# The entry of a gate/up stage: five blocks begun ahead of the left factors, weights prepared by GpSimd, normed rows kept in the projection's tile

## The chip, the cores and the metric

The kernel runs on one core of a Trainium2 chip, in one launch. The metric is the device time of one execution in microseconds. A core has TensorE (PE, matmuls out of SBUF into PSUM), VectorE (DVE), ScalarE (ACT), GpSimd (POOL) and SyncE (SP, which issues most DMAs here). Each works off its own list of instructions in order, and waits on semaphores where it needs another's result.

## The reference

One layer of a streaming encoder on 512 tokens of width 2048, all float32: four token mixers side by side, cross-attention into 256 memory tokens, and a SwiGLU feed-forward of width 5632, each between two RMS norms.

```python
def swiglu_ffn(h, w_gu, w_down):
    gate, up = jnp.split(h @ w_gu, 2, axis=-1)
    return (jax.nn.silu(gate) * up) @ w_down
...
        x = x + rmsnorm(xa, g[XA_POST])
        x = x + rmsnorm(swiglu_ffn(rmsnorm(x, g[FFN_PRE]), ffn_w_gu[l], ffn_w_down[l]), g[FFN_POST])
```

The change lies between the last projection of the attention (which gives `xa`) and the first product of `h @ w_gu`.

## The kernel before

Every float32 factor is split in two parts for TensorE: a high part in the rounded format fp32r, made by a cast on ScalarE (names `whi`, `L` first half), and a low part, source minus high part, made by a subtraction on VectorE (`wlo`, `L` second half). `split3` (L991, L992) does this for one tile of 128 x 1024.

The attention's output projection is `y_proj`. It leaves its result in the tile `y` (four row tiles of 128 tokens, 2048 wide). It runs for the token tiles in two pairs, 0 and 1, then 2 and 3. After each pair, `advance_t` adds the residual (L953, the new x goes to DRAM at L956 by a DMA on GpSimd's queue), takes the squares for the next norm (`sumsq`, L242, on ScalarE), finds the inverse root by a row of small VectorE operations (L148 to L153; "root" below), scales the rows (L963 on ScalarE, L964 on VectorE), and transposes them on TensorE through PSUM (L970). VectorE evicts the transposes with the norm's gain (L972) into the tiles `xT` (named `stg`, `sa12` and so on).

`gate_up` computes h @ w_gu by a scheme with seven products in place of eight, on halves of the inner dimension, of the tokens, and of gate and up. Products are numbered 1 to 7. Each takes a left factor (`L[m]`, the tokens' side: a half of `xT` or a sum of halves, split in two parts) and a right factor (a half of a weight block or a sum of halves). The output's 5632 columns go in 44 blocks `j` of 128. One product of a block is 16 matmuls (`product`, L1088 and L1090, a high part by 512 columns and a low part by 256, eight times). A block's products 1 and 2 only need the first pair of token tiles (L1, L2), so they can be done before the second pair is normed: `begin(j)` does that and finishes the gate's first half, through one tile `f_x`. It holds one of the five PSUM banks named `mm` until `block(j)` takes over with products 6, 5, 7, 3 and 4. Three blocks are begun in `phase2` (pool `early`), blocks 3 and 4 inside `gate_up`.

Block 0 is run in steps together with the left factors 5, 6, 7, 4 and 3 (`left_parts`: four sums for each of two halves, then `split3`), since its own products use them first. Its right factors come from `right_parts` (sums at L1030, L1033, L1035, L1037) and `split_w`. Raw weights come by SP's queue, 512 KB a tile, into rings of three.

The order on each engine is set by a scheduler that interleaves the emitted instructions; the code gives the dependencies and the order of emission. The pools give how far something can run ahead.

Of the kernel before, what the change touches and what calls it, by code (L numbers as in the profile page):

```python
# [7 lines left out]
F32 = mybir.dt.float32  # L8
# [7 lines left out]
P = 128  # L16
# [53 lines left out]
def build(tc, x, mem, norm_g, w_in, conv_a_w, pool_w, pool_scale, gdn_conv_w, gdn_A_log,  # L70
# [824 lines left out]
    def phase2(act):  # L895
        with ExitStack() as s0:
            pp = pool("ptp", stack=s0)
            pt = [tuple(pp.tile([P, 4, T], F32R, name=f"pt{s}{i}") for s in "hl") for i in range(2)]
            with ExitStack() as s1:
                pl = pool("atp", stack=s1)  # L900
                for h in range(XH):
                    qh = pl.tile([P, 4, T], F32R, name="at_qh", bufs=2)
                    ql = pl.tile([P, 4, T], F32R, name="at_ql", bufs=2)
                    proj_a(act, xa_wq, h * XHD, lambda j, o: split(qh[:, j], ql[:, j], o), 2)
                    ks = slice(2 * (h % 2), 2 * (h % 2) + 2)
                    attention(h, qh, ql, pl, pt[h // 2][0][:, ks], pt[h // 2][1][:, ks])
                    if h == 0:
                        value_out(3, pl)
            es_act.close()
            ep = pool("early", 2, "right", es_early)  # L910
            sa12 = pool("sa12", 2, "right", es_a12)
            sa22 = pool("sa22", 2, "right", es_a22)
            stg = pool("stg", 4, "right", es_stg)
            yp = pool("yp2", stack=s0)
            pl2 = pool("adp2", stack=s0)
            xT = [[[p.tile([P, 4, 256], F32, name="stg") for _ in range(2)] for p in q]
                  for q in ((stg, stg), (sa12, sa22))]
            L = {m: [ep.tile([P, 4, 2, 256], F32R, name=f"L{m}") for _ in range(2)] for m in (1, 2)}
            begun = {}

            def then(i):
                def f(y, ss):
                    advance_t((2 * i, 2 * i + 1), y, ss, xT, pl2)
                    if i == 0:
                        for sub in range(2):
                            split3(pair(L[1][sub]), xT[0][0][sub])
                            split3(pair(L[2][sub]), xT[1][0][sub])
                    else:
                        for j in range(3):
                            begun[j] = begin(j, L, ep)  # L930
                return f
            y_proj(pt, vw_d, 3, yp, [(0, range(NT), None)] + [
                (c, range(2 * i, 2 * i + 2), then(i) if c == 3 else None) for i in range(2) for c in (1, 2, 3)])
        return xT, L, begun

    def advance_t(tiles, y, ss, xT, pl):


        xs = []
        for t in tiles:  # L940
            xt = pl.tile([P, D], F32, name="ad_x", bufs=2)
            nc.sync.dma_start(xt, x1_d[t * P:(t + 1) * P])
            xs.append(xt)
        s = sm.tile([P, 2], F32, name="rs_s")
        for i, t in enumerate(tiles):
            nc.vector.tensor_reduce(s[:, i:i + 1], ss[:, t], axis=AX.X, op=ALU.add)
        r = sm.tile([P, 2], F32, name="rs_r")
        mean_rsqrt(r, s, 2, D)
        sq = sm.tile([P, 2, 2], F32, name="nr_q")
        for i, t in enumerate(tiles):  # L950
            for hf in range(2):
                qs = slice(hf * 1024, (hf + 1) * 1024)
                nc.vector.scalar_tensor_tensor(xs[i][:, qs], y[:, t, qs], r[:, i:i + 1], xs[i][:, qs],  # L953
                                               op0=ALU.mult, op1=ALU.add)
                sumsq(xs[i][:, qs], sq[:, i, hf:hf + 1], pl)
            nc.gpsimd.dma_start(x2_d[t * P:(t + 1) * P], xs[i])  # L956
        s2 = sm.tile([P, 2], F32, name="nr_s2")
        nc.vector.tensor_reduce(s2, sq, axis=AX.X, op=ALU.add)
        n = sm.tile([P, 2], F32, name="nr_r2")
        mean_rsqrt(n, s2, 2, D)  # L960
        for hf in range(2):
            qs = slice(hf * 1024, (hf + 1) * 1024)
            nc.scalar.activation(xs[0][:, qs], xs[0][:, qs], AF.Copy, scale=n[:, 0:1])  # L963
            nc.vector.tensor_scalar(xs[1][:, qs], xs[1][:, qs], n[:, 1:2], None, op0=ALU.mult)  # L964
        for q in (0, 2, 1, 3):
            for i, t in enumerate(tiles):
                tp = ps.tile([P, 4, P], F32, name="ps")
                for j in range(4):
                    k = q * 4 + j
                    nc.tensor.transpose(tp[:, j], xs[i][:, k * P:(k + 1) * P], ident)  # L970
                o = t % 2 * P
                nc.vector.tensor_tensor(xT[q // 2][t // 2][q % 2][:, :, o:o + P], tp,  # L972
                                        bc(PA[:, 5 * 16 + q * 4:5 * 16 + q * 4 + 4], P), op=ALU.mult)

# [5 lines left out]

    ORDER = (1, 2, 6, 5, 7, 3, 4)
    FIRST = (5, 6, 7, 4, 3)

    def pair(t):

        return t[:, :, 0], t[:, :, 1]

    def split3(hl, src):  # L990
        nc.scalar.copy(hl[0], src)  # L991
        nc.vector.tensor_tensor(hl[1], src, hl[0].bitcast(F32), op=ALU.subtract)  # L992

    def left_parts(A11, A12, A21, A22, tmp, L, order):

# [24 lines left out]
                sums(3)  # L1020
            yield m

    def right_parts(B11, B12, B21, B22, new, order):

        tt = nc.vector.tensor_tensor
        s = {}
        for m in order:
            if m in (5, 6) and 5 not in s:
# [11 lines left out]
    def gate_up(xT, L, begun):  # L1040

        with ExitStack() as s0:
            def factor(name, *ms):
                lp = pool(name, 2, stack=s0, reuse_waits="tile")
                for m in ms:
# [6 lines left out]
            parts = [left_parts(xT[0][0][sub], xT[1][0][sub], xT[0][1][sub], xT[1][1][sub],  # L1052
                                tmp.tile([P, 4, 256], F32, name="tmp"),
                                Lazy(lambda m, sub=sub: pair(L[m][sub])), FIRST) for sub in range(2)]
            first = block(0, L, rp, tp, begun[0], FIRST)

            def step():
                for g in parts:
# [1 line left out]
                next(first)  # L1060
            step()
            step()
            begun[3] = begin(3, L, tp)
            step()
            es_stg.close()
            es_tmp.close()
            factor("lp4", 4)
            step()
            begun[4] = begin(4, L, tp)
            es_a22.close()  # L1070
            factor("lp3", 3)
            step()
# [19 lines left out]
    def fold(dst, src):  # L1092
        nc.vector.tensor_tensor(dst, src[:, 0:256], src[:, 256:512], op=ALU.add)

    def split_w(src):
        w = wp.tile([P, 8, P], F32R, name="whi"), wp.tile([P, 8, P], F32R, name="wlo")
        split3(w, src)
        return w

    def begin(j, L, pl):  # L1100


        A = mm.tile([P, 512], F32, name="mm")
        X, g = pl.tile([P, T], F32, name="f_x", bufs=1), pl.tile([P, 256], F32, name="f_g", bufs=3)
        for m, kh in ((2, 1), (1, 0)):
            b = wp.tile([P, 8, P], F32, name="raw")
            nc.sync.dma_start(b, w_gu[j, kh, 0])
            product(A, split_w(b), L, m)
            if m == 2:
                nc.scalar.copy(X, A)  # L1110
        gate(g, A, X)
# [7 lines left out]
        nc.scalar.activation(th, g, AF.Tanh, scale=0.5)  # L1119
        nc.vector.scalar_tensor_tensor(g, th, 1.0, g, op0=ALU.add, op1=ALU.mult)  # L1120

    def block(j, L, rp, tp, begun, order):

        q = {}
        for kh, g in ((0, 0), (1, 0), (0, 1), (1, 1)):
# [1 line left out]
            nc.sync.dma_start(q[kh, g], w_gu[j, kh, g])  # L1127
        tl = lambda n, w=T: tp.tile([P, w], F32, name="f_" + n, bufs=1)
        parts = right_parts(q[0, 0], q[0, 1], q[1, 0], q[1, 1], lambda: tp.tile([P, 8, P], F32, name="sum"),
                            (() if begun else (1, 2)) + order)  # L1130
        if begun:
            A, g = begun
        else:
# [8 lines left out]
        h = tl("h")  # L1142
        tt, stt = nc.vector.tensor_tensor, nc.vector.scalar_tensor_tensor
        for m in order:
            product(bank[m], split_w(next(parts)), L, m)
            if m == 5:
                Z = tl("z")
                nc.scalar.copy(Z, Cc)
# [244 lines left out]
```

## Time and profile before

| | |
|---|---|
| time, median of 3 runs | 2781.76 us (2767.03 to 2784.7) |
| profiled execution | 2785.32 us |
| its span on the core | 2783.5 us |
| granted TensorE clock, mean | 0.988 |
| busy share PE / DVE / ACT / POOL | 97% / 70% / 45% / 5% |

Times are read from the span's start. "Busy" of TensorE counts pipelined matmuls, so that a busy PE need not be at its peak. A row of the timeline gives start, duration, engine, source line, operation, the tiles written and read, shapes and count; in brackets the idle time of the engine before it and what ended that. Where a row merges several instructions (x4), its duration runs from the first one's start to the last one's end.

### The profile page before, as it was taken

To read this page: it belongs to the slowest core of one execution; us is meant where nothing else is said; L and a number is where in the kernel's file an instruction comes from. 1 tells how busy PE (TensorE), PEld (TensorE's weight loads), DVE (VectorE), ACT (ScalarE), POOL (GpSimd) and SP (SyncE) were. 2 spreads that over 40 slices of the span, in tenths; PEclk is the share of its full clock that TensorE was granted. 3 is DMA by queue.
4 is the path that set the end of the run, shared out by engine and by line. 5 is a ranking of instruction groups with operands and counts; after the bars stand their busy time and mean duration, and the time that the engine had idled before them with its cause. 6 is when DMAs were issued, how large, how long until landed. Compare 5 with 4: busy or idle time off the path is not lost. (4 is left out here: it accounts for less than half of the span.)

```text
span 2783.5 us, 35244 instructions
## 1 busy us (share of the span) xinstructions
PE 2695.7 (97%) x13426; PEld 2250.9 (81%) x13426; DVE 1946.2 (70%) x2869; ACT 1265.0 (45%) x1918; POOL 139.4 (5%) x219
## 2 busy tenths in 40 slices
PE   8999999999999999999979999999999998999997
PEld 6788788878778877888757888888888887888885
DVE  5735557456762355334689988888888889999966
ACT  5623423233452245433554545454544455555542
POOL 0000001100000001000000000000000000000002
PEclk9999999999999999999989999999999999999998
DMA  8632322344675368533644333333334336577656
GB/s 290 235 103 85 94 69 85 109 129 126 220 259 198 98 210 289 167 98 107 203 166 161 123 118 122 118 123 116 125 114 128 112 113 234 197 191 189 174 118 236
DMA packets 158755, 428.08 MB, mean 154 GB/s; under 512 B 18157, under 2 KB 29306, under 8 KB 147706
## 3 DMA queue, kind: packets, MB, share of 16 engines
q1 hardware_dynamic: 140154, 355.57, 39.3%
q0 software_dynamic: 18432, 70.27, 8.7%
q8 instruction: 105, 1.72, 0.3%
q14 instruction: 64, 0.52, 0.1%
HBM read 351.30 MB, written 74.47 MB: 153 GB/s over the span
## 5 line engine op out<-in xcount | busy, mean ns | idle before, releaser
L1088 PE MATMUL mm<-L,whi 128*128 128x512 f32 x1448 | 524.9, 403 | 14.1 <-ACT f_x L1110 7.6
L162 DVE SCALAR_TENSOR_TENSOR wlo<-raw,PA,whi 128x512 fp32r<-128x512 f32 x368 | 263.1, 747 | 301.0 <-ACT whi L161 300.8
L161 ACT ACTIVATE whi<-raw,PA 128x512 fp32r<-128x512 f32 x368 | 247.8, 718 | 399.4 <-PE mm L178 213.2
L1090 PE MATMUL mm<-L,wlo 128*128 128x256 f32 x1448 | 410.2, 284 | 5.7 <-DVE wlo L992 5.7
L1088 PE MATMUL ps<-L,whi 128*128 128x512 f32 x1016 | 364.7, 398 | 0.0
L1088 PEld LDWEIGHTS mm<-L,whi 128*128 128x128 f32 x1448 | 275.3, 190 | 84.3 <-ACT f_x L1110 8.5
L177 PE MATMUL mm<-act,whi 128*128 128x512 f32 x832 | 330.3, 397 | 0.0
L179 PE MATMUL mm<-act,wlo 128*128 128x512 f32 x832 | 327.4, 394 | 0.0
L178 PE MATMUL mm<-act,whi 128*128 128x512 f32 x832 | 326.8, 393 | 0.0
L1090 PE MATMUL ps<-L,wlo 128*128 128x256 f32 x1016 | 285.4, 281 | 0.1
L1090 PEld LDWEIGHTS mm<-L,wlo 128*128 128x128 f32 x1448 | 277.0, 191 | 8.8 <-DVE wlo L992 8.5
L991 ACT CAST whi<-raw 128x1024 fp32r<-128x1024 f32 x176 | 185.0, 1052 | 187.0 <-PE ps L1088 112.9
L177 PE MATMUL mm<-whi,act 128*128 128x512 f32 x640 | 251.9, 394 | 2.2 <-ACT act L158 1.6
L178 PE MATMUL mm<-wlo,act 128*128 128x512 f32 x640 | 251.1, 393 | 2.0 <-DVE wlo L162 2.0
L179 PE MATMUL mm<-whi,act 128*128 128x512 f32 x640 | 250.5, 392 | 0.2 <-DVE act L159 0.2
L159 DVE TENSOR_TENSOR wlo<-raw,whi 128x1024 fp32r<-128x1024 f32 x92 | 112.3, 1224 | 193.8 <-ACT whi L158 193.6
L1088 PEld LDWEIGHTS ps<-L,whi 128*128 128x128 f32 x1016 | 190.9, 188 | 47.4
L992 DVE TENSOR_TENSOR wlo<-raw,whi 128x1024 fp32r<-128x1024 f32 x176 | 214.1, 1217 | 6.2 <-ACT whi L991 6.2
L992 DVE TENSOR_TENSOR wlo<-sum,whi 128x1024 fp32r<-128x1024 f32 x132 | 161.6, 1224 | 75.0 <-ACT whi L991 74.9
L991 ACT CAST whi<-sum 128x1024 fp32r<-128x1024 f32 x132 | 138.3, 1051 | 145.9 <-PE mm L1088 65.5
L1090 PEld LDWEIGHTS ps<-L,wlo 128*128 128x128 f32 x1016 | 191.9, 189 | 0.5 <-DVE wlo L992 0.4
L158 ACT CAST whi<-raw 128x1024 fp32r<-128x1024 f32 x92 | 96.9, 1053 | 189.3 <-PE mm L179 143.4
(505 smaller groups left out, 4940.9 us busy)
## 6 DMA issues: line engine op xcount, KB each, us to landing
raw<-in_w_gu_dram SPq DMA_DIRECT2D x186, 512.0 KB, 3.5
raw<-in_w_in_dram SPq DMA_DIRECT2D x88, 512.0 KB, 3.6
rawB<-in_w_down_dram SPq DMA_DIRECT2D x40, 1024.0 KB, 5.5
raw<-in_xa_wkv_dram SPq DMA_DIRECT2D x64, 512.0 KB, 4.6
raw<-in_w_out_dram SPq DMA_DIRECT2D x32, 512.0 KB, 3.9
raw<-in_xa_wo_dram SPq DMA_DIRECT2D x32, 512.0 KB, 6.2
raw<-in_xa_wq_dram SPq DMA_DIRECT2D x32, 512.0 KB, 4.1
raw<-vw_d SPq DMA_DIRECT2D x28, 512.0 KB, 4.3
```

Of the source, the lines that this page charges most:

```text
L158: nc.scalar.copy(hi, src)
L159: nc.vector.tensor_tensor(lo, src, hi.bitcast(F32), op=ALU.subtract)
L161: nc.scalar.activation(hi, src, AF.Copy, scale=scale)
L162: nc.vector.scalar_tensor_tensor(lo, src, scale, hi.bitcast(F32), op0=ALU.mult, op1=ALU.subtract)
L177: nc.tensor.matmul(o, ah, bh, start=start, stop=False, skip_group_check=reopen)
L178: nc.tensor.matmul(o, ah, bl, start=False, stop=False, skip_group_check=reopen)
L179: nc.tensor.matmul(o, al, bh, start=False, stop=stop, skip_group_check=reopen)
L991: nc.scalar.copy(hl[0], src)
L992: nc.vector.tensor_tensor(hl[1], src, hl[0].bitcast(F32), op=ALU.subtract)
L1088: nc.tensor.matmul(bank, wh[:, k], t.rearrange("p s n -> p (s n)"), start=k == 0 and m in (1, 2, 5), stop=k == 7, **kw)
L1090: nc.tensor.matmul(bank[:, 0:256], wl[:, k], t[:, 0], start=False, stop=k == 7, **kw)
```

## The change

`BEGUN = 5`: all five blocks are begun in `phase2`, behind the second pair's `advance_t`, and none in `gate_up`. The low parts of the begun blocks' weights (ten subtractions), and the four sums and five low parts of block 0's right factors, are given to GpSimd instead of VectorE. In `advance_t` the squares (thrown away) and then the normed rows are written into `y`, which the residual has read by then, so that the tile `ad_x` stays as it is for its DMA. Of each pair of transposes the first is evicted by ScalarE in four pieces of 128 x 128, the second by VectorE as before. What is computed is the same.

```diff
-                        for j in range(3):
+                        for j in range(BEGUN):
                             begun[j] = begin(j, L, ep)
...
-                sumsq(xs[i][:, qs], sq[:, i, hf:hf + 1], pl)
+                nc.scalar.activation(y[:, t, qs], xs[i][:, qs], AF.Square, accum_out=sq[:, i, hf:hf + 1])
...
-            nc.scalar.activation(xs[0][:, qs], xs[0][:, qs], AF.Copy, scale=n[:, 0:1])
-            nc.vector.tensor_scalar(xs[1][:, qs], xs[1][:, qs], n[:, 1:2], None, op0=ALU.mult)
+            nc.scalar.activation(y[:, tiles[0], qs], xs[0][:, qs], AF.Copy, scale=n[:, 0:1])
+            nc.vector.tensor_scalar(y[:, tiles[1], qs], xs[1][:, qs], n[:, 1:2], None, op0=ALU.mult)
...
-                    nc.tensor.transpose(tp[:, j], xs[i][:, k * P:(k + 1) * P], ident)
+                    nc.tensor.transpose(tp[:, j], y[:, t, k * P:(k + 1) * P], ident)
                 o = t % 2 * P
-                nc.vector.tensor_tensor(xT[q // 2][t // 2][q % 2][:, :, o:o + P], tp,
-                                        bc(PA[:, 5 * 16 + q * 4:5 * 16 + q * 4 + 4], P), op=ALU.mult)
+                dst = xT[q // 2][t // 2][q % 2][:, :, o:o + P]
+                if i == 0:
+                    for j in range(4):
+                        nc.scalar.activation(dst[:, j], tp[:, j], AF.Copy, scale=gcol(5, q * 4 + j))
+                else:
+                    nc.vector.tensor_tensor(dst, tp, bc(PA[:, 5 * 16 + q * 4:5 * 16 + q * 4 + 4], P), op=ALU.mult)
...
+    BEGUN = 5
...
-    def split3(hl, src):
+    def split3(hl, src, eng=None):
         nc.scalar.copy(hl[0], src)
-        nc.vector.tensor_tensor(hl[1], src, hl[0].bitcast(F32), op=ALU.subtract)
+        (eng or nc.vector).tensor_tensor(hl[1], src, hl[0].bitcast(F32), op=ALU.subtract)
...
-    def right_parts(B11, B12, B21, B22, new, order):
+    def right_parts(B11, B12, B21, B22, new, order, eng=None):
 
-        tt = nc.vector.tensor_tensor
+        tt = (eng or nc.vector).tensor_tensor
...
-            first = block(0, L, rp, tp, begun[0], FIRST)
+            first = block(0, L, rp, tp, begun[0], FIRST, nc.gpsimd)
...
             step()
             step()
-            begun[3] = begin(3, L, tp)
             step()
             es_stg.close()
             es_tmp.close()
             factor("lp4", 4)
             step()
-            begun[4] = begin(4, L, tp)
...
-        X, g = pl.tile([P, T], F32, name="f_x", bufs=1), pl.tile([P, 256], F32, name="f_g", bufs=3)
+        X, g = pl.tile([P, T], F32, name="f_x", bufs=1), pl.tile([P, 256], F32, name="f_g", bufs=BEGUN)
...
-            product(A, split_w(b), L, m)
+            product(A, split_w(b, nc.gpsimd), L, m)
...
-            product(bank[m], split_w(next(parts)), L, m)
+            product(bank[m], split_w(next(parts), eng), L, m)
```

Line numbers from L972 on move by up to five in the new kernel: L977 is the eviction of transposes that VectorE keeps, L997 the subtraction, L1010 to L1020 the left sums, L1035 to L1042 the right sums, L1119 to L1123 the gate of a begun block, L1174 the store of h.

GpSimd's list between the attention and the middle of the gate/up stage, before:

```order
L891 DMA vw_d<-at_e 128x512 x3
L767 DMA x_d<-ad_x 128x2048
L891 DMA vw_d<-at_e 128x512 x21
L956 DMA x_d<-ad_x 128x2048 x4
L1171 DMA h_d<-f_h 128x512 x44
```

And now, from the first pair's stores of x (`ISA` sets the engine up for its arithmetic):

```order
L956 DMA x_d<-ad_x 128x2048 x2
L997 ISA
L997 TENSOR_TENSOR wlo<-raw,whi 128x1024 x4
L956 DMA x_d<-ad_x 128x2048 x2
L997 TENSOR_TENSOR wlo<-raw,whi 128x1024 x6
L1035 TENSOR_TENSOR sum<-raw 128x1024
L1038 TENSOR_TENSOR sum<-sum,raw 128x1024
L1040 TENSOR_TENSOR raw<-raw 128x1024
L997 TENSOR_TENSOR wlo<-sum,whi 128x1024 x2
L1042 TENSOR_TENSOR sum<-sum,raw 128x1024
L997 TENSOR_TENSOR wlo<-raw,whi 128x1024
L997 TENSOR_TENSOR wlo<-sum,whi 128x1024
```

A last low part of a raw block and the stores of h follow. The second pair's stores stand behind the weights of the first two begun blocks, the other three blocks' and all of block 0's behind those stores.

VectorE's list from the eviction of the second pair's transposes on, before (`L_11433` and `L_11434` are left factor 5 of the two halves):

```order
L964 TENSOR_SCALAR ad_x<-ad_x,nr_r_11202 128x1024 x2
L972 TENSOR_TENSOR stg<-ps,PA 128x4x128 x8
L1116 TENSOR_TENSOR f_x<-mm,f_x 128x512
L1005 TENSOR_TENSOR tmp<-stg 128x1024
L1093 TENSOR_TENSOR f_g<-f_x 128x256
L1005 TENSOR_TENSOR tmp<-stg 128x1024
L992 TENSOR_TENSOR L_11433<-tmp,L_11433 128x4x256
L1120 SCALAR_TENSOR_TENSOR f_g<-f_x,f_g 128x256
L992 TENSOR_TENSOR L_11434<-tmp,L_11434 128x4x256
L1030 TENSOR_TENSOR sum<-raw 128x1024
L1012 TENSOR_TENSOR stg<-stg 128x1024 x2
L992 TENSOR_TENSOR wlo<-sum,whi 128x1024
```

And now (`L_11553` and `L_11554` are left factor 5):

```order
L964 TENSOR_SCALAR y<-ad_x,nr_r_11206 128x1024 x2
L977 TENSOR_TENSOR stg<-ps,PA 128x4x128 x2
L1010 TENSOR_TENSOR tmp<-stg 128x1024
L977 TENSOR_TENSOR stg<-ps,PA 128x4x128 x2
L1119 TENSOR_TENSOR f_x<-mm,f_x 128x512
L1010 TENSOR_TENSOR tmp<-stg 128x1024
L1096 TENSOR_TENSOR f_g<-f_x 128x256
L997 TENSOR_TENSOR L_11553<-tmp,L_11553 128x4x256
L1123 SCALAR_TENSOR_TENSOR f_g<-f_x,f_g 128x256
L1017 TENSOR_TENSOR stg<-stg 128x1024
L997 TENSOR_TENSOR L_11554<-tmp,L_11554 128x4x256
L1014 TENSOR_TENSOR stg<-tmp,stg 128x1024
```

Four of the eight evictions and the right factors of block 0 are gone from here, and the left sums stand closer together. Further on, three sums of block 1 (L1035, L1040, L1038) stand ahead of left factor 3, the last one of block 0.

On TensorE the ten begun products, which before lay partly between block 0's, now all stand ahead of block 0's product 6, but for the last of them, which follows it. Block 0 ends with 11 matmuls of product 3, the 16 of product 4, and the other 5 of product 3, and then block 1's product 6 begins; before, it ended with 15 of product 3. On SP's list the loads of blocks 3 and 4 stand ahead of nearly all loads of block 0.

More of the change, by code (lines that the diff above doesn't have):

```diff
@@ L1093, in fold, with split_w @@
         nc.vector.tensor_tensor(dst, src[:, 0:256], src[:, 256:512], op=ALU.add)
-    def split_w(src):
+    def split_w(src, eng=None):
         w = wp.tile([P, 8, P], F32R, name="whi"), wp.tile([P, 8, P], F32R, name="wlo")
-        split3(w, src)
+        split3(w, src, eng)
         return w
@@ L1120, in gate, with block @@
         nc.vector.scalar_tensor_tensor(g, th, 1.0, g, op0=ALU.add, op1=ALU.mult)
-    def block(j, L, rp, tp, begun, order):
+    def block(j, L, rp, tp, begun, order, eng=None):
         q = {}
@@ L1129, in block @@
         parts = right_parts(q[0, 0], q[0, 1], q[1, 0], q[1, 1], lambda: tp.tile([P, 8, P], F32, name="sum"),
-                            (() if begun else (1, 2)) + order)
+                            (() if begun else (1, 2)) + order, eng)
         if begun:
```

## The prediction

> **What bounds the kernel now.** I read the page's first line, then a table by stage around the place of the change (columns: stretch and length in us, then busy time with instruction counts of PE, PEld, DVE, ACT and POOL, granted TensorE clock, DMA share, GB/s), then who waits for whom on PE there, then the timelines of PE, DVE, ACT and POOL.
>
> ```profile
> span 2783.5 us, 35244 instructions
> 1421.20:1441.30 20.10, 15.37 (x80) 12.45 (x78) 16.49 (x34) 9.36 (x14) 1.06 (x2) 0.83 0.71 262
> 1441.30:1470.00 28.70, 17.23 (x64) 13.40 (x64) 28.70 (x31) 14.36 (x18) 0.00 (x0) 0.70 0.17 57
> 1470.00:1489.50 19.50, 18.10 (x98) 14.96 (x98) 17.72 (x23) 11.61 (x15) 0.00 (x0) 1.00 0.52 159
> 1489.50:1520.00 30.50, 28.78 (x162) 24.74 (x163) 28.14 (x36) 14.17 (x19) 1.10 (x2) 1.00 0.45 156
> 1600.00:1700.00 100.00, 100.00 (x568) 86.68 (x567) 88.42 (x111) 50.06 (x67) 2.70 (x5) 1.00 0.39 121
> ```
>
> The steady gate/up stage (last row) is TensorE's: never idle, 568 matmuls in 100 us, 0.176 us each, so a product of 16 matmuls takes 2.82 us. The entry is different: from 1441.3 to 1470 VectorE is busy without a break, TensorE idles 11.5 us of 28.7 and is granted 0.70 of its clock, and DMA moves little (0.17).
>
> ```profile
> PE mm L1088 <- ACT f_x L1110: 7.6, 3, 6.5
> PE mm L1088 <- ACT whi L991: 6.2, 3, 5.2
> PE mm L1090 <- DVE wlo L992: 4.0, 4, 2.7
> 1414.98 0.39 PE L1088 MATMUL mm<-L,whi 128*128 128x512 f32 x1
> 1488.87 0.39 PE L1088 MATMUL mm<-L,whi 128*128 128x512 f32 x1
> L970 PE MATMUL ps<-C,ad_x 128*128 128x128 f32 x64 | 10.3, 309 | 2.2 <-ACT ad_x L963 2.0
> ```
>
> The first three rows are TensorE's waits between 1415 and 1490 (total, times, longest), 17.8 us; each ends a chain through VectorE. The next two are the first matmul of the first begun block and the first of block 1. Between them stand 240 matmuls of products and 32 transposes: 42.2 us at 0.176, and some 5 us, half of the last row's 10.3. So 47 us of work took 73.9: at most 27 us are to be had, 1.0% of the kernel.
>
> **The change, part by part.** VectorE's prices in the entry:
>
> ```profile
> 1421.24 4.87 DVE L953 SCALAR_TENSOR_TENSOR ad_x<-y,rs_r,ad_x 128x1024 f32<-128x1024 f32 x4
> 1429.63 0.16 DVE L237 TENSOR_SCALAR mr_v<-nr_s 128x2 f32<-128x2 f32 x1
> 1431.81 0.16 DVE L153 SCALAR_TENSOR_TENSOR nr_r<-rsq_t,nr_r 128x2 f32<-128x2 f32 x1
> 1435.16 1.41 DVE L964 TENSOR_SCALAR ad_x<-ad_x,nr_r 128x1024 f32<-128x1024 f32 x2 [3.20 <-DMA x_d<-ad_x]
> L972 DVE TENSOR_TENSOR stg<-ps,PA 128x512 f32<-128x512 f32 x16 | 10.2, 684 | 1.4 <-PE ps L970 1.4
> 1448.22 2.35 DVE L1012 TENSOR_TENSOR stg<-stg 128x1024 f32<-128x1024 f32 x2
> L1093 DVE TENSOR_TENSOR f_g<-f_x 128x256 f32<-128x256 f32 x44 | 18.4, 417 | 0.0
> 1483.12 1.21 DVE L992 TENSOR_TENSOR wlo<-raw,whi 128x1024 fp32r<-128x1024 f32 x1
> ```
>
> Two 128x1024 operations take 2.35 us and one 1.21, so each costs 1.13 in a row (by the same overlap of 0.08, a 128x256 one 0.34 and an L972 0.6). The last row is the last factor that block 0 needed; it ended at 1484.3.
>
> Nineteen of these 128x1024 operations go to GpSimd: ten low parts of begun blocks, four sums and five low parts of block 0. VectorE is freed of 19 x 1.13 = 21.5 us. GpSimd does the same kind of operation only in the last stage, at half the width (the POOL rows below): three in 3.80 us, 1.27 each. I take twice that, 2.54 us, for 128x1024. The bounds are 1.27, were all of it fixed cost, and 3.5, should the rounding to fp32r, which no GpSimd row shows, cost a good third more. Nineteen come to 48 us.
>
> ```profile
> 2734.53 3.80 POOL L1334 TENSOR_TENSOR y<-y,gB 128x512 f32<-128x512 f32 x3 [18.34 <-ACT yjk L1328]
> 2734.97 0.69 DVE L1326 TENSOR_TENSOR y<-mm,y 128x512 f32<-128x512 f32 x1 [0.69 <-PE mm L179]
> 2739.53 1.29 POOL L1334 TENSOR_TENSOR y<-y,gB 128x512 f32<-128x512 f32 x1 [1.20 <-ACT yjk L1328]
> 2740.06 0.78 DVE L151 TENSOR_TENSOR rsq_t<-rs_r 128x1 f32<-128x1 f32 x1
> 2741.26 0.16 DVE L151 TENSOR_TENSOR rsq_t<-rs_r 128x1 f32<-128x1 f32 x1
> 2754.67 3.77 DVE L1340 SCALAR_TENSOR_TENSOR ad_x<-y,rs_r,ad_x 128x512 f32<-128x512 f32 x4
> 2754.85 1.71 POOL L1334 TENSOR_TENSOR y<-y,gB 128x512 f32<-128x512 f32 x1 [2.79 <-ACT yjk L1328]
> 2776.96 2.74 DVE L1340 SCALAR_TENSOR_TENSOR ad_x<-y,rs_r,ad_x 128x512 f32<-128x512 f32 x4 [0.15 <-DVE rs_r L153]
> ```
>
> These rows decide the case. A one-element operation of VectorE that takes 0.16 took 0.78 when it started inside a GpSimd operation, and ended with it (2740.84 against 2740.82). Four L1340 took 3.77 beside a GpSimd operation and 2.74 without one; there the GpSimd operation, begun 0.18 us after the first L1340, took 1.71, not 1.29. L1326, which reads one operand from PSUM, ran in 0.69 inside a GpSimd operation. So a VectorE operation with two operands in SBUF and a GpSimd one exclude each other and take turns where both have a queue; only those that read PSUM run beside. Nearly all that VectorE keeps in the entry has two SBUF operands. The longest hold in these rows is 1.0 us (3.77 less 2.74), by operations half as long as here; I take the hold to last as long as the operation. The Trainium skill, SBUF — State Buffer, "Who interferes with whom", speaks against this change: one of the two gets the shared port pair for its whole instruction and the other fully blocks. By that rule the bill below stands; were a hold to end at the 1.0 us that the rows show, 15 x 1.5 = 23 us would leave it, and the change would win some 7.
>
> Now the bill of the shared port, from the second pair's L953 on, which starts at 1421.2 less 0.8 (below), 1420.4. GpSimd's first four operations come before it, where VectorE was not full. The other fifteen stand behind the L956 stores, which wait for L953: 15 x 2.54 = 38.1. VectorE with two SBUF operands: L953 4.9; the second root 2.3 (1429.63 to 1431.97); L964 1.4; eight sums and ten low parts of the left factors, 18 x 1.13 = 20.3; folds and gates of four begun blocks and one fold, 9 x 0.34 = 3.1; three sums of block 1, which now stand ahead of block 0's last left factors, 3.4. Together 35.4. The sum is 73.5 us, to 1493.9. Behind that point TensorE has 32 matmuls before block 1 (the rest of L3's product and all of L4's), 5.6 us: block 1 starts at 1499.5, against 1488.9. That is +10.6 with a port that is never idle. In the same stretch VectorE idled 3.6 and 1.8 us before (20.10 less 16.49, 19.50 less 17.72); I add 5 for the new one: +15.6. The bounds are 0 and 12 us of idle port: on top of the 5, four casts on ScalarE that wait for a GpSimd sum, 1.05 each by the row below, and four L972 at 0.6. That gives +10.6 to +22.6. A clock of 0.70, as in the stalled stretch, over the last 5.6 us would add 2.4.
>
> ```profile
> L991 ACT CAST whi<-sum 128x1024 fp32r<-128x1024 f32 x132 | 138.3, 1051 | 145.9 <-PE mm L1088 65.5
> raw<-in_w_gu_dram SPq DMA_DIRECT2D x186, 512.0 KB, 3.5
> ```
>
> Another width of the term stands in the Trainium skill: GPSIMD Engine Reference, "3.1 Elementwise — side-by-side cycle accounting", has 4497 ns for an addition of 2048 elements; with 1.27 at 512 that makes an estimate of 2.35 us at 1024, and a bill 2.9 us shorter. No run here shows it.
>
> Beginning five blocks adds no matmul, since blocks 3 and 4 were begun inside the entry anyway. It gives TensorE two more blocks (four products, 11.3 us) that need no new left factor, and that would cover the waits of 6.5 and 5.2, if their weights came. They wait for GpSimd, though, in whose queue they stand ahead of block 0's nine operations; those are late next. On SP's queue four loads of 512 KB move ahead of block 0's loads; the DMA share of 0.17 hides them, and without that cover a load costs the 3.5 us of the row above. Queued behind GpSimd's work is the store of block 0's h, for which nobody waits in this stage.
>
> Putting the normed rows into y removes the 3.20 us wait of L964 for the store of x2. TensorE had a begun product to do then, so it is worth nothing by itself, and the bill holds no such wait. The squares go into y instead of a scratch tile, at the same price.
>
> ScalarE's evictions take four L972 (2.4 us) from VectorE in each pair and give ScalarE 16 small copies.
>
> ```profile
> L1164 ACT COPY f_t<-mm x44: 361/366/372, 1482.2 to 2320.9; 128x256 f32<-128x256 f32 x44
> 1395.46 1.05 ACT L991 CAST L<-stg 128x1024 fp32r<-128x1024 f32 x1 [0.36 <-DVE stg L972]
> 1397.38 1.05 ACT L991 CAST L<-stg 128x1024 fp32r<-128x1024 f32 x1 [0.87 <-DVE stg L972]
> 1400.04 2.20 ACT L158 CAST whi<-raw 128x1024 fp32r<-128x1024 f32 x2
> 1404.27 3.48 DVE L159 TENSOR_TENSOR wlo<-raw,whi 128x1024 fp32r<-128x1024 f32 x3
> 1405.53 0.50 PE L178 MATMUL mm<-wlo,pth 128*128 128x512 f32 x1 [3.93 <-DVE wlo L159]
> ```
>
> A 128x256 copy is 0.37, so a 128x128 one some 0.22: 3.5 us on ScalarE ahead of the casts at 1400.04, 1.2 of it in place of its waits for L972. The first of those casts then ends by 1403.4 and its low part can start up to 0.9 earlier than 1404.27. In the first pair I take 0.8 us earlier; the bounds are 3.9 (the whole wait goes) and 1.2 later. In the second pair ScalarE has room (9.36 us of 20.1).
>
> After block 1 has begun, the 1.7 us that TensorE idled in 1489.5:1520 may go, since VectorE is three sums ahead: I take 1.1 back.
>
> **The rivals.** First, the port does not bind, because holds are as short as those seen. Then GpSimd's own queue sets the end: 1425.3 (L953's end) + 38.1 + 5 to 12 of hand-overs + 5.6 = 1474 to 1481, that is 8 to 15 us before 1488.9; about -10, 2772 us. For it: the rows show short holds only. Against it: they end together with the GpSimd operation.
>
> Second, a GpSimd operation costs more than twice L1334. At 3.5 us the fifteen add 15 x 0.96 = 14.4 to the forecast's 14.5: +29, 2811 us. It passes 1% from 3.4 us an operation. For it: no GpSimd row writes fp32r. Against it: on VectorE such rows cost the same (1.21 for L992, 2.35 for two L1012).
>
> Third, a draw: much of GpSimd's 1.27 is fixed cost, and 128x1024 takes 1.6. Fifteen times 0.94 is 14.1, the whole forecast: -4 to +4, 2782 us. For it: the trace has one width only. Against it: VectorE's prices (0.42, 0.68, 1.21 for 256, 512 and 1024) are mostly by element.
>
> **How the numbers follow.** 15.6 - 1.1 = +14.5 (the 0.8 is in the start). The profiled execution took 2785.3, so it would be 2799.8; it lies 3.5 above the median of the runs shown, 2781.8, to which I apply the sum: 2796. The forecast's own range is +6 (10.6 less 1.7, and the first pair's bound 3.1 better) to +27 (22.6, 2.4 for the clock and 2.0 for the first pair), 2788 to 2809. About 1%, 28 us, is what a measurement of this kernel tells from no change. Chances: forecast 0.72, port does not bind 0.12, dearer GpSimd 0.08, draw 0.08. The range takes in the draw and most of the first rival and ends at the second: 2774 to 2811. Slower by over 1% is the second rival and the forecast's edge, 0.10. Faster by over 1% needs more than the 27 us there are, or the runs' scatter of 17 on top of the first rival: 0.03. Within 1%: 0.87.
>
> **What would show it.** GpSimd's 128x1024 rows at 2.5 us, up to 3.7 where they start inside a VectorE operation; low parts and sums of left factors on VectorE at 1.2 to 3.7 us; root operations of 2 us; TensorE waiting for GpSimd's wlo; block 1 beginning some 90 us after the first begun matmul, not 74. The forecast is wrong if VectorE's operations keep 1.2 us beside GpSimd's, or if block 1 begins within 74 us.

## The result, and the profile after

The changed kernel takes 2797.83 us (median of 7 runs, 2789.38 to 2798.44), the kernel before 2781.76 us (7 runs, 2767.03 to 2785.47). The ratio is 1.0051, with a 95% interval from 1.003 to 1.0072: slower by half a per cent, some 14 us. The profiled execution has a span of 2796.5 us.

The runs of one and the same kernel lie in two groups some 14 us apart, the profiles put that difference behind the entry (from block 5's gate to the last store of h they show 754 or 768 us), and the share of runs in the lower group differs between kernels (7 of 35 for the kernel before, 6 of 12 for e_rows_ev and 10 of 12 for e_begun_gp below), so a few microseconds are better read from the entry's rows than from two medians or a ratio.

First the table by stage, from the first matmul of a begun block to the first of block 1 and from there to the gate of block 5, the first block that is not begun. The columns are those of the prediction's table. Of the kernel before:

```profile
1414.98:1488.87 73.89, 56.29 (x274) 45.80 (x272) 67.62 (x101) 37.98 (x50) 1.06 (x2) 0.84 0.44 150
1488.87:1555.57 66.70, 64.30 (x359) 54.58 (x358) 61.61 (x78) 30.89 (x41) 2.72 (x5) 1.00 0.42 144
```

Of the changed kernel:

```profile
1413.73:1504.05 90.32, 58.41 (x274) 47.07 (x273) 81.08 (x79) 41.24 (x65) 49.11 (x20) 0.79 0.38 126
1504.05:1566.82 62.77, 62.12 (x355) 53.80 (x354) 60.27 (x77) 30.39 (x43) 2.74 (x5) 1.00 0.47 154
```

The first row of each pair is the case in one line. VectorE now has 79 instructions where it had 101, and is busy for 81.08 us where it was for 67.62. GpSimd's part took work away from it and made the rest slower. Block 1 begins 90.3 us after the first begun matmul, not 73.9, that is 15.2 us later in the execution; 3.9 us of it are made up by block 5's gate (66.70 against 62.77), which stands 11.3 us later. The two matmuls that mark the stretch, from TensorE's timeline of the changed kernel:

```profile
1413.73 0.39 PE L1091 MATMUL mm<-L,whi 128*128 128x512 f32 x1
...
1504.05 0.40 PE L1091 MATMUL mm<-L,whi 128*128 128x512 f32 x1
```

TensorE's longest waits between them (total, times, longest):

```profile
PE mm L1091 <- ACT f_x L1113: 19.1, 4, 7.5
PE ps L1091 <- ACT whi L996: 5.9, 1, 5.9
PE mm L1091 <- ACT whi L996: 3.2, 1, 3.2
PE mm L1093 <- POOL wlo L997: 2.5, 2, 1.3
```

They name ScalarE's copy `f_x`, but ScalarE had long been free: the copy waits until VectorE has read the tile for the begun block before. GpSimd's and VectorE's timelines show why that is late. GpSimd, changed kernel:

```profile
1415.70 4.73 POOL L997 TENSOR_TENSOR wlo<-raw,whi 128x1024 fp32r<-128x1024 f32 x2 [0.95 <-ACT whi L996]
...
1427.98 2.35 POOL L997 TENSOR_TENSOR wlo<-raw,whi 128x1024 fp32r<-128x1024 f32 x1
1432.08 2.37 POOL L997 TENSOR_TENSOR wlo<-raw,whi 128x1024 fp32r<-128x1024 f32 x1 [1.75 <-ACT whi L996]
1442.12 2.42 POOL L997 TENSOR_TENSOR wlo<-raw,whi 128x1024 fp32r<-128x1024 f32 x1 [7.67 <-ACT whi L996]
...
1455.88 2.70 POOL L997 TENSOR_TENSOR wlo<-raw,whi 128x1024 fp32r<-128x1024 f32 x1 [1.76 <-ACT whi L996]
1458.54 3.33 POOL L1035 TENSOR_TENSOR sum<-raw 128x1024 f32<-128x1024 f32 x1
1461.94 2.42 POOL L1038 TENSOR_TENSOR sum<-sum,raw 128x1024 f32<-128x1024 f32 x1
1464.33 3.32 POOL L1040 TENSOR_TENSOR raw<-raw 128x1024 f32<-128x1024 f32 x1
1467.61 3.32 POOL L997 TENSOR_TENSOR wlo<-sum,whi 128x1024 fp32r<-128x1024 f32 x1
...
1494.74 3.15 POOL L997 TENSOR_TENSOR wlo<-raw,whi 128x1024 fp32r<-128x1024 f32 x1 [2.59 <-ACT whi L996]
```

VectorE, changed kernel:

```profile
1415.71 2.39 DVE L148 TENSOR_SCALAR rs_r<-mr_v 128x2 int32<-128x2 int32 x1
1418.13 2.33 DVE L149 TENSOR_SCALAR rs_r<-rs_r 128x2 int32<-128x2 int32 x1
...
1422.26 4.87 DVE L953 SCALAR_TENSOR_TENSOR ad_x<-y,rs_r,ad_x 128x1024 f32<-128x1024 f32 x4
...
1432.23 2.23 DVE L153 SCALAR_TENSOR_TENSOR nr_r<-rsq_t,nr_r 128x2 f32<-128x2 f32 x1
...
1435.68 1.42 DVE L964 TENSOR_SCALAR y<-ad_x,nr_r 128x1024 f32<-128x1024 f32 x2
...
1456.26 0.68 DVE L1119 TENSOR_TENSOR f_x<-mm,f_x 128x512 f32<-128x512 f32 x1
...
1459.59 2.57 DVE L1096 TENSOR_TENSOR f_g<-f_x 128x256 f32<-128x256 f32 x1
1462.07 6.65 DVE L997 TENSOR_TENSOR L<-stg,L 128x1024 fp32r<-128x1024 f32 x2
1468.65 2.55 DVE L1123 SCALAR_TENSOR_TENSOR f_g<-f_x,f_g 128x256 f32<-128x256 f32 x1
...
1498.09 1.21 DVE L997 TENSOR_TENSOR L<-stg,L 128x1024 fp32r<-128x1024 f32 x1
```

Read the two lists side by side between 1461.9 and 1471.2. GpSimd's L1038 holds the first L997 until 1464.36; that runs 1.1 us, during which L1040 waits; L1040 then runs its 2.2 us and holds the second L997; that runs, and so on. The two engines take turns, one instruction each. The 128x256 operation L1123, 0.42 us alone, ends at 1471.20 behind all that, the copy `f_x` (L1113) starts at 1471.24, and TensorE, idle for 7.49 us by then, goes on at 1471.88. The small operations of the root suffer most: L153, 128x2 and 0.16 us before, takes 2.23 where it meets a GpSimd instruction, and L148 and L149 ahead of L953 take 2.39 and 2.33, as long as GpSimd's instruction does. In the kernel before, L148 was:

```profile
1418.03 0.16 DVE L148 TENSOR_SCALAR rs_r<-mr_v 128x2 int32<-128x2 int32 x1
```

L1119, which has one operand in PSUM, runs in 0.68 inside a GpSimd instruction.

### The profile page after: what moved, and what is told of

It is laid out like the page before. It is cut to its first block, busy times and chain, and to the rows that moved or that the text cites. A ratio compares the mean times of both kernels' runs of the same rounds, so it can differ in the third digit from the quotient of the medians.

```text
span 2796.5 us, 35277 instructions
## 1 busy us (share of the span) xinstructions
PE 2698.1 (96%) x13426; PEld 2253.2 (81%) x13426; DVE 1953.5 (70%) x2842; ACT 1272.5 (46%) x1950; POOL 191.3 (7%) x238
## 5 line engine op out<-in xcount | busy, mean ns | idle before, releaser
L1091 PE MATMUL mm<-L,whi 128*128 128x512 f32 x1448 | 526.3, 404 | 22.7 <-ACT f_x L1113 19.1
L996 ACT CAST whi<-raw 128x1024 fp32r<-128x1024 f32 x176 | 185.1, 1052 | 185.6 <-PE ps L1091 113.8
L159 DVE TENSOR_TENSOR wlo<-raw,whi 128x1024 fp32r<-128x1024 f32 x92 | 112.3, 1224 | 192.6 <-ACT whi L158 192.3
L997 DVE TENSOR_TENSOR wlo<-sum,whi 128x1024 fp32r<-128x1024 f32 x129 | 158.0, 1225 | 75.9 <-ACT whi L996 75.9
L996 ACT CAST whi<-sum 128x1024 fp32r<-128x1024 f32 x132 | 138.5, 1051 | 146.8 <-PE mm L1091 80.2
L997 DVE TENSOR_TENSOR wlo<-raw,whi 128x1024 fp32r<-128x1024 f32 x164 | 199.7, 1218 | 1.3 <-ACT whi L996 1.2
L179 PEld LDWEIGHTS mm<-act,wlo 128*128 128x128 f32 x832 | 156.7, 188 | 32.1 <-issue 0.5
```

Source lines behind the costliest of these rows:

```text
L159: nc.vector.tensor_tensor(lo, src, hi.bitcast(F32), op=ALU.subtract)
L179: nc.tensor.matmul(o, al, bh, start=False, stop=stop, skip_group_check=reopen)
L997: (eng or nc.vector).tensor_tensor(hl[1], src, hl[0].bitcast(F32), op=ALU.subtract)
L1091: nc.tensor.matmul(bank, wh[:, k], t.rearrange("p s n -> p (s n)"), start=k == 0 and m in (1, 2, 5), stop=k == 7, **kw)
```

## The experiments

Eleven kernels were run, each against the kernel before on the same chip. Three theories stand against each other: S, the shared port, the prediction's; Q, GpSimd's own list of instructions is what ends last, whatever VectorE does; X, the single tile `f_x`, which the waits name. "Block 1" and "block 5" are the times from the first begun matmul to block 1's first matmul and to block 5's gate, read from the profiles.

| kernel | ratio to before [95%] | block 1, us | block 5, us |
|---|---|---|---|
| before | 1 | 73.9 | 140.6 |
| changed | 1.0051 [1.003, 1.0072] | 90.3 | 153.1 |
| e_vec | 0.9973 [0.9952, 0.9993] | 71.9 | 138.5 |
| e_set | 0.9957 [0.9937, 0.9978] | 75.5 | 137.9 |
| e_x5 | 1.0047 [1.0027, 1.0066] | 90.3 | 156.9 |
| e_dup | 1.0091 [1.0067, 1.0114] | 100.3 | 166.3 |
| e_half | 1.0035 [1.0017, 1.0054] | 87.1 | 155.1 |
| e_begun_gp | 0.9979 [0.9956, 1.0001] | 76.4 | 141.3 |
| e_b0_gp | 1.001 [0.9988, 1.0031] | 77.6 | 143.8 |
| e_gp3 | 1.0029 [1.0014, 1.0045] | 82.5 | 147.7 |
| e_rows_ev | 0.9968 [0.9947, 0.9988] | 71.6 | 138.2 |
| e_rows | 1.0005 [0.999, 1.002] | 73.1 | 140.1 |
| e_vec_x5 | 0.9978 [0.9959, 0.9996] | 71.8 | 136.4 |

**The GpSimd part taken out of the changed kernel (e_vec).**

```diff
-            first = block(0, L, rp, tp, begun[0], FIRST, nc.gpsimd)
+            first = block(0, L, rp, tp, begun[0], FIRST)
...
-            product(A, split_w(b, nc.gpsimd), L, m)
+            product(A, split_w(b), L, m)
```

> All weights of begun blocks and of block 0 back on VectorE; five begun blocks, rows in y and ScalarE's evictions stay. Three theories. S, the shared port: a GpSimd operation (2.4 us) and a VectorE one with two SBUF operands exclude each other. Q, GpSimd's own queue: its nineteen slow operations in a row set the end, whatever VectorE does. X, the single tile f_x: with five blocks begun in a row, TensorE's waits on f_x (19.1 us in the changed kernel's page) set the end. S and Q: the fifteen operations behind L953 cost 15 x 1.13 = 17 us of VectorE in place of 36 us, less what TensorE then waits for: 12 to 16 us under the changed kernel, 2782 to 2786. X: within 3 us of the changed kernel's 2798.

The ratio is 0.9973, and the stretch to block 5 falls from 153.1 to 138.5 us. That is 2774 us on the kernel before's 2781.76, some 8 below what S and Q expected and 24 below X. Its row by stage:

```profile
1415.24:1487.18 71.94, 56.95 (x274) 46.73 (x272) 65.49 (x97) 41.35 (x67) 1.06 (x2) 0.86 0.46 157
```

With 97 instructions VectorE is busy for 65.5 us, 15.6 less than with the 79 of the changed kernel. All that the change lost, and a little more, comes from GpSimd's part; whether by S or by Q this run doesn't tell.

**GpSimd as busy, but hardly reading (e_set).** GpSimd's two lines are L1001 and L1003 here, and the lines behind them are six higher than in the changed kernel.

```diff
-        (eng or nc.vector).tensor_tensor(hl[1], src, hl[0].bitcast(F32), op=ALU.subtract)
+        if eng is None:
+            nc.vector.tensor_tensor(hl[1], src, hl[0].bitcast(F32), op=ALU.subtract)
+        else:
+            lo = hl[1].bitcast(F32)
+            eng.tensor_tensor(hl[1][:, :, 0:1], src[:, :, 0:1], hl[0][:, :, 0:1].bitcast(F32), op=ALU.subtract)
+            for _ in range(2):
+                eng.memset(lo[:, :, 1:], 0.0)
```

> Left out: GpSimd's subtractions compute 8 of 1024 elements per row; in place of the rest the low part is set to zero twice, so that GpSimd is busy a like time (two fills of 1016 elements, 2.1 us by the 0.54 us of a 512 fill on the page) but reads next to nothing. Block 0's sums stay on GpSimd. S: beside the fills VectorE's operations keep 1.2 and 0.42 us, only the four sums still hold them; block 1 begins near where the first rival of the prediction had it, 2772 to 2782. Q: GpSimd's queue is as long as before, 2792 to 2798. X: 2795 to 2798.

A low part costs GpSimd 0.21 + 2 x 0.95 = 2.1 us here, nearly the 2.4 of the changed kernel, in much the same list and behind the same stores. The ratio is 0.9957 (2770 us, 2 below S's range and 22 below Q's) and the stretch to block 5 is 137.9, as without GpSimd. Q falls as an account of the loss: its list is nearly as long, and the time is gone. One thing besides the reads differs, though: a fill needs no result of ScalarE's cast, so it can run ahead of it (the row of 1446.85 below waited for TensorE), where the changed kernel's subtractions wait for `whi`. So it is this run together with the rows of held operations that speaks for S. GpSimd in this kernel:

```profile
1429.29 2.71 POOL L1003 MEMSET wlo<- 128x1016 f32 x3
...
1446.85 1.96 POOL L1003 MEMSET wlo<- 128x1016 f32 x2 [12.79 <-PE mm L1099]
...
1466.42 2.50 POOL L1046 TENSOR_TENSOR raw<-raw 128x1024 f32<-128x1024 f32 x1
```

VectorE in this kernel:

```profile
1429.19 2.83 DVE L237 TENSOR_SCALAR mr_v<-nr_s 128x2 f32<-128x2 f32 x1
...
1447.44 1.22 DVE L1016 TENSOR_TENSOR tmp<-stg 128x1024 f32<-128x1024 f32 x1
...
1466.57 3.43 DVE L1041 TENSOR_TENSOR sum<-raw 128x1024 f32<-128x1024 f32 x1
```

A two-operand operation keeps its 1.22 us inside two memsets, and takes 3.43 beside one of the four sums, which GpSimd still reads and writes in full. That is what S says. By the Trainium skill, SBUF — State Buffer, "Who interferes with whom", a VectorE instruction with two SBUF inputs contends with a GpSimd instruction that reads SBUF, not with one that only writes; these rows agree. The first row of each list is another case: a one-operand TENSOR_SCALAR of 128x2, 0.17 us elsewhere, took 2.83 beside three memsets.

**Block 0's low parts computed twice (e_dup).**

```diff
-            product(bank[m], split_w(next(parts), eng), L, m)
+            src = next(parts)
+            w = split_w(src, eng)
+            if eng is not None:
+                eng.tensor_tensor(w[1], src, w[0].bitcast(F32), op=ALU.subtract)
+            product(bank[m], w, L, m)
```

> The changed kernel with each of block 0's five low parts computed twice on GpSimd, into the same tile. S: five operations of 2.4 more, each with a turn of VectorE's of up to 1.2 in it, all behind the point from which the port is full: 12 to 18 us more, 2810 to 2816. Q: 5 x 2.4 = 12 us more, 2810. X: 0 to 5 us more, 2798 to 2803.

Five more GpSimd operations of 2.4 us, 12 us in all, move block 1 by 10.0 us and the ratio to 1.0091.

```profile
1413.84:1514.12 100.28, 56.74 (x274) 46.04 (x273) 92.02 (x79) 42.33 (x66) 63.32 (x25) 0.81 0.34 115
```

VectorE has the same 79 instructions and is busy for 92.0 us instead of 81.1. Each GpSimd operation costs nearly its whole length. The 13.2 us to block 5 (166.3 against 153.1) lie within S's 12 to 18, the ratio's 2807 us a little below. Q expected nearly the same, so of the three only X is hit.

**A tile of its own for each begun block instead of `f_x` (e_x5).**

```diff
-                            begun[j] = begin(j, L, ep)
+                            begun[j] = begin(j, L, ep, y[:, j // 4, j % 4 * 512:j % 4 * 512 + 512])
...
-        X, g = pl.tile([P, T], F32, name="f_x", bufs=1), pl.tile([P, 256], F32, name="f_g", bufs=BEGUN)
+        g = pl.tile([P, 256], F32, name="f_g", bufs=BEGUN)
```

> The changed kernel with a tile of its own in place of f_x for each of the five begun blocks (rows of y that are no longer needed). S and Q: TensorE then waits for GpSimd's low parts in place of f_x, at most 4 us better than 2798. X: most of the 19 us of waits on f_x go, 2780 to 2786.

TensorE's waits in the same stretch of this kernel:

```profile
PE mm L1093 <- POOL wlo L997: 10.3, 4, 4.6
PE ps L1091 <- DVE L L997: 5.7, 1, 5.7
PE mm L1091 <- ACT y L1113: 4.9, 2, 4.2
```

Of the 19.1 us of waits for that copy 4.9 are left (it goes into `y` now), waits for low parts of GpSimd and VectorE stand in their place, and block 1 comes after the same 90.3 us. X falls: it expected 2780 to 2786 us, and the ratio makes 2795; the wait was a symptom. (Block 5 stands at 156.9 only because the stretch starts 3.9 us sooner in this run; its gate starts at 1566.75, against 1566.82.)

**GpSimd's instructions cut in two (e_half).**

```diff
-        (eng or nc.vector).tensor_tensor(hl[1], src, hl[0].bitcast(F32), op=ALU.subtract)
+        if eng is None:
+            nc.vector.tensor_tensor(hl[1], src, hl[0].bitcast(F32), op=ALU.subtract)
+        else:
+            for h in (slice(0, 4), slice(4, 8)):
+                eng.tensor_tensor(hl[1][:, h], src[:, h], hl[0][:, h].bitcast(F32), op=ALU.subtract)
```

> The changed kernel, with each low part that GpSimd makes (128x1024) cut in two instructions of 128x512; the work is the same. Theory S, with a hold as long as GpSimd's instruction: VectorE's 128x1024 rows in the entry fall from 3.4 us (1.2 and a hold of 2.2 to 2.4) to about 2.4 (1.2 and a hold of 1.2), a row of 128x2 of the root to 1.3 us at most, and GpSimd's low parts come later, since VectorE gets two turns where it had one. The sum of the port's work grows only by the fixed cost of 15 more instructions, 15 x 0.15 = some 2 us, so the stretch from the first begun product to block 5's gate stays at 153 to 157 us and the ratio at 1.004 to 1.007. If it is VectorE's left factors, not the port's sum, that end last, the stretch falls to 146 to 150. A hold of a fixed length, whatever the instruction, would leave the root's rows at 2.2 us and lengthen the stretch by about 15 x 1 us, to 165.

The four halves in this kernel's GpSimd timeline that meet the root of the second pair:

```profile
1414.95 5.03 POOL L1001 TENSOR_TENSOR wlo<-raw,whi 128x512 fp32r<-128x512 f32 x4 [0.81 <-ACT whi L996]
```

And that root in its VectorE timeline:

```profile
1414.97 1.30 DVE L148 TENSOR_SCALAR rs_r<-mr_v 128x2 int32<-128x2 int32 x1
1416.31 1.22 DVE L149 TENSOR_SCALAR rs_r<-rs_r 128x2 int32<-128x2 int32 x1
1417.56 1.20 DVE L151 TENSOR_TENSOR rsq_t<-rs_r 128x2 f32<-128x2 f32 x1
1418.79 1.21 DVE L152 SCALAR_TENSOR_TENSOR rsq_t<-rsq_t,mr_v 128x2 f32<-128x2 f32 x1
```

Four holds of 1.2 us where the changed kernel had two of 2.35. A hold lasts as long as the GpSimd instruction, and the sum stays: 155.1 us to block 5, against 153.1, as expected (the ratio, 1.0035, is a little below the expected 1.004). Block 1 itself comes 3.2 us sooner, which fits VectorE's two turns where it had one, but block 5's gate does not keep it.

**The two halves of GpSimd's work (e_begun_gp, e_b0_gp).** The first leaves it the ten low parts of the begun blocks:

```diff
-            first = block(0, L, rp, tp, begun[0], FIRST, nc.gpsimd)
+            first = block(0, L, rp, tp, begun[0], FIRST)
```

> The changed kernel with block 0's sums and low parts back on VectorE; GpSimd keeps the ten low parts of begun blocks. S: nine of the fifteen operations behind L953 cost 1.13 in place of 2.4 of the port, 9 x 1.27 = 11 us less: 2785 to 2789. Q: GpSimd's queue ends after ten, 2782 to 2786.

The second leaves it block 0's four sums and five low parts:

```diff
-            product(A, split_w(b, nc.gpsimd), L, m)
+            product(A, split_w(b), L, m)
```

> The changed kernel with the ten low parts of begun blocks back on VectorE; GpSimd keeps block 0's four sums and five low parts. S: six of the fifteen operations behind L953 cost 1.13 in place of 2.4, and the root's small operations are no longer held by the first four: 8 to 11 us less, 2787 to 2791. Q: nine operations in a row, 22 us, can start as soon as block 0's weights are there, so GpSimd is done before TensorE needs it: 2778 to 2784.

By the ratios both expectations missed: e_begun_gp comes to 2776 us, below S and Q alike, and e_b0_gp to 2784.5, between the two. In the entry, the better measure here (e_begun_gp's ratio is below 1 though its entry is 0.7 us longer than the kernel before's), they lie 11.8 and 9.3 us below the changed kernel, where S had 11 and 8 to 11.

To block 5 they take 2.8 and 5.3 us more than e_vec, and both together, in the changed kernel, 14.6. The bill of the port gives a reason why the sum is more than its parts. I count it as the prediction did, from the second pair's L953 on, with 35.4 us for what VectorE has in any case, 1.13 for each operation of the fifteen that is VectorE's, and 2.38 (the middle of the undisturbed rows 2.35 to 2.42) for each that is GpSimd's:

| kernel | GpSimd's, VectorE's | bill, us | over e_vec | block 1 over e_vec, measured |
|---|---|---|---|---|
| e_vec | 0, 15 | 52.4 | 0 | 0 |
| e_begun_gp | 6, 9 | 59.9 | 7.5 | 4.4 |
| e_b0_gp | 9, 6 | 63.6 | 11.2 | 5.7 |
| changed | 15, 0 | 71.1 | 18.7 | 18.4 |
| e_dup | 20, 0 | 83.0 | 30.6 | 28.3 |

Of the small bills 3.1 and 5.5 us find idle time; the large ones are paid nearly in full. e_set, with 4 sums and a bill of 44.9, does not fit the table: its bill is the smallest, and its block 1 is 3.6 us later than e_vec's, though block 5's gate is not. The bill leaves out that the fills hold the one-operand rows of its second root (L237, L148 and L149 there take 4.8 us in place of 0.5); whether that is all of it was not tried.

**One part alone, in the kernel before (e_gp3, e_rows_ev, e_rows).** e_gp3 has the GpSimd lines of the change with three begun blocks (the helpers take the engine as in the change):

```diff
-            first = block(0, L, rp, tp, begun[0], FIRST)
+            first = block(0, L, rp, tp, begun[0], FIRST, nc.gpsimd)
...
-            product(A, split_w(b), L, m)
+            product(A, split_w(b, nc.gpsimd), L, m)
```

> The kernel before with the GpSimd part of the change alone: three blocks begun early and two inside, rows in place, VectorE's evictions. S: the whole bill stands, since the same nineteen operations are moved: 12 to 20 us over the kernel before, 2794 to 2802. X: the chain of f_x is as before, so no more than 5 us over it, 2782 to 2787.

It alone costs 7.1 us to block 5 (147.7 against 140.6), ratio 1.0029. That lies between S's 12 to 20 and X's 5 at most; S had expected the whole bill here, and it did not come. The changed kernel loses 12.5, although its evictions gain some 2 (below) and five begun blocks without GpSimd cost nothing (e_vec against e_rows_ev). So some 7 us arise where both come together: then all ten low parts of begun blocks stand ahead of block 0's nine operations in GpSimd's list, and three sums of block 1 ahead of left factors in VectorE's. Which of the two it is was not tried.

e_rows_ev has the rows in `y` and ScalarE's evictions, e_rows only the rows. The lines that they share (the evictions of e_rows_ev are as in the change):

```diff
-                sumsq(xs[i][:, qs], sq[:, i, hf:hf + 1], pl)
+                nc.scalar.activation(y[:, t, qs], xs[i][:, qs], AF.Square, accum_out=sq[:, i, hf:hf + 1])
...
-            nc.scalar.activation(xs[0][:, qs], xs[0][:, qs], AF.Copy, scale=n[:, 0:1])
-            nc.vector.tensor_scalar(xs[1][:, qs], xs[1][:, qs], n[:, 1:2], None, op0=ALU.mult)
+            nc.scalar.activation(y[:, tiles[0], qs], xs[0][:, qs], AF.Copy, scale=n[:, 0:1])
+            nc.vector.tensor_scalar(y[:, tiles[1], qs], xs[1][:, qs], n[:, 1:2], None, op0=ALU.mult)
...
-                    nc.tensor.transpose(tp[:, j], xs[i][:, k * P:(k + 1) * P], ident)
+                    nc.tensor.transpose(tp[:, j], y[:, t, k * P:(k + 1) * P], ident)
```

> The kernel before with normed rows and squares in y and half the transposes evicted by ScalarE; three blocks begun early, no GpSimd arithmetic. By the prediction's terms: 0.8 us from the first pair, four L972 of 0.6 in the second pair on a VectorE that is full there (2.4), and nothing for L964's wait: 1 to 4 us under the kernel before, 2778 to 2781. If L964's wait of 3.2 us was on the path: 5 to 8 us under it.

> The kernel before with the squares and the normed rows written into y, and nothing else (VectorE evicts all transposes). If the gain of the run with both (0.9968, stretch 138.2) came from the rows, since the scaling no longer waits 3.2 us for the store of x: ratio 0.997, stretch from the first begun product to block 5's gate 138 us. If it came from ScalarE's evictions: ratio 1.000, stretch 140 to 141. My prediction had the rows at nothing and the evictions at 0.8 us.

The rows alone give 1.0005, nothing, and 0.5 us in the entry. With the evictions it is 0.9968 and 2.4 us in the entry, so about 1.9 us come from the evictions. The ratio speaks of 9 us. Some 4 of them come from the two shares named in the result (6 of 12 against 7 of 35 is 0.3 more, of 14 us); the rest beyond the 2.4 is not found in the entry, and I leave it open. Against e_rows_ev, e_vec adds the five begun blocks: 138.5 against 138.2 us, so beginning five blocks ahead by itself gives nothing.

**The rest together (e_vec_x5):** the changed kernel without GpSimd's part, and with the tiles of e_x5.

> The changed kernel with all weights back on VectorE (0.9973, stretch 138.5) and a tile of its own in place of f_x for each begun block. TensorE's waits for ScalarE's f_x in the entry of that kernel are 5.1 us, the longest 2.7. If the single tile was what they waited for, the stretch falls to 134 to 136 and the ratio to 0.995 to 0.996; if they wait for VectorE's queue ahead of f_x, it stays at 138 to 139 and the ratio at 0.997.

The stretch to block 5 is 136.4 us, the shortest of all, 2.1 less than e_vec and short of the 134 to 136 expected if the tile was all that TensorE waited for; the ratio of 0.9978 is no better than that of e_vec or e_rows_ev. These three are 2.1 to 4.2 us, some 0.1%, shorter than the kernel before in the entry. Their ratios, 0.2 to 0.3% below 1, do not tell the three apart.

## Why the prediction was right

The forecast was 2796 us, +14.5 on the kernel before; 2797.83 was measured, and the ratio makes +14.2. Its steps:

- **The shared port binds, and a hold lasts as long as GpSimd's instruction.** Right. e_set takes GpSimd's reads away and with them the loss, and e_half halves the holds. The row that decides for the whole length against the 1.0 us of the older rows is L148 with 2.39. The rival in which the port does not bind (2772 us, block 1 at 1474 to 1481) falls. That e_set's runs, where the reads of the low parts are gone, have a median of 2768 us does not bear it out: block 1 starts at 1488.4 there.
- **Operations with two SBUF operands are held, and only those that read PSUM run beside.** Not exact. L148 and L149 have one SBUF operand, and at 128x2 they were held. At 128x1, in the kernel before, the same line kept its price inside the GpSimd instruction of 2739.53 to 2740.82; what makes the difference was not tried:

```profile
2739.68 0.15 DVE L148 TENSOR_SCALAR rs_r<-rs_s 128x1 int32<-128x1 int32 x1
```

- **GpSimd's operation at 2.54 us.** Mis-sized by 0.16: undisturbed rows are 2.35 to 2.42, which is 2.4 us on fifteen. The estimate of 2.35, worked out from the Trainium skill, GPSIMD Engine Reference, "3.1 Elementwise — side-by-side cycle accounting", was the nearer one; these rows agree with it. Writing fp32r costs nothing extra: L1038, which writes float32, took 2.42 too. The dearer GpSimd and the draw fall with these rows.
- **The start of the second L953, 1420.4.** Wrong: 1422.26. I had left the first four GpSimd operations out of the bill as lying where VectorE was not full. Two of them (1415.70, 4.73 us) hold L148 and L149 of the root ahead of L953, 2.39 and 2.33 where 0.16 each were due. So the step "first four operations come before it" failed by some 2 us.
- **The port's idle time, 5 us.** From 1422.26 to the end of the last left factor (1498.09 + 1.21 = 1499.30) are 77.0 us; the bill at measured prices is 71.1, which leaves 5.9. This is a remainder by the bill's prices, not a measured time.
- **Block 1 at 1499.5 + 5 = 1504.5.** It began at 1504.05: the start 1.9 later, GpSimd 2.4 cheaper, 0.9 more idle time, and 4.75 us behind the last factor where I had 5.6. That the number is so close is luck: errors of both signs cancel, the largest of them 2.4.
- **1.1 us back after block 1.** Mis-sized: 3.9. TensorE's idle time in that stretch fell from 2.40 us (66.70 less 64.30) to 0.65, which makes 1.75 of it; the other 2.2 is not attributed. So block 5's gate came 11.3 us later, where the steps have 14.5. The two spans differ by 13.0; the remaining 1.7 lies behind the gate, where the prediction had nothing. That the ratio's 14.2 comes so near to 14.5 is luck too.
- **The first pair, -0.8.** Cannot be told. From the first transpose to the first begun matmul the kernel before took 23.3 us and the changed one 24.9; the ten kernels with ScalarE's evictions lie between 22.1 and 25.0, the three without between 21.9 and 23.3. One of ScalarE's 128x128 evictions takes 0.25 us in a row, where I had 0.22.
- **Rows in y at nothing.** Right: L964 does not wait any more (1435.68, no idle time ahead of it), and e_rows shows no gain.
- **Two more begun blocks as cover for TensorE.** Right that their weights wait for GpSimd; the waits for `f_x`, 19.1 us, were not foreseen as the place where it would show, since I looked at low parts. e_x5 shows that the place does not matter.

## What to carry to other kernels

Work moved from VectorE to GpSimd is not work done beside VectorE: where VectorE's remaining instructions read two operands from SBUF, add both engines' lists into one, with GpSimd's at 2.1 times VectorE's price, before calling anything freed. Where a profile's first symptom is a wait for some third thing, as here for a copy on ScalarE, compare the engine's busy time with its count of instructions: fewer instructions and more busy time was the sign of a lock here. A lock of this kind costs small operations most, so keep chains of 128x2 operations clear of long GpSimd instructions; cutting those in two only spread the same holds over twice as many operations in e_half.

## What the runs showed of the hardware

- With both lists full, VectorE and GpSimd alternate one instruction each (rows from 1461.94 on): neither is starved, and both look slower by the other's length, 3.4 and 3.3 us where 1.2 and 2.4 are their own.
- A GpSimd memset does not hold a two-operand VectorE operation (1.22 us inside it), but holds a one-operand TENSOR_SCALAR of 128x2 (0.17 us alone, 2.83 beside three memsets).
- A 128x1024 subtraction cut in two instructions of 128x512 takes GpSimd about 2.5 us, for 2.4 in one (four halves in 5.03, against two wholes in 4.73): the cut costs 0.15 us, and halves each hold.
